# A decoder layer with 32 routed experts: the second block of a large expert set one unit behind the first, and the tokens of the next expert turned in two places

## The chip, the cores and the metric

The kernel runs on one core of a Trainium2 chip. The metric is the device time of one execution in microseconds (us); the change is made to a kernel of 1811.78 us (median of three runs).

## What is computed

One layer over 512 tokens of 1024 features: a mixer (gated DeltaNet and differential attention), a top-4-of-32 mixture of experts, and a gated embedding, each followed by a layer norm. Only the mixture is touched. Each expert that a token chose is a clamped SwiGLU:

```python
hgu = xb @ w_gu[e] + b_gu[e]                     # 1024 -> 2048
gate = jnp.minimum(hgu[:, :D_FF], 7.0)
up = jnp.clip(hgu[:, D_FF:], -7.0, 7.0)
act = (up + 1.0) * gate * jax.nn.sigmoid(1.702 * gate)
return act @ w_down[e] + b_down[e]               # 1024 -> 1024
```

The result is scaled by the token's gate and added to the token's row. How many tokens an expert has depends on the data.

## The kernel before, in words

**Units.** The weights of an expert are twelve units of 1 MB: 0 to 7 of `w_gu` (two row halves for each of four column blocks), 8 to 11 of `w_down`. Twelve raw buffers `mr` form a ring that SP fills (`mload`, L838); a buffer is loaded again when its unit has been split. ACT rounds a unit to its high part (`hi_of`, L1204, tile `mh`), DVE takes the rest (`lo_of`, L1209, tile `ml`); four pairs of such tiles form a second ring. `ahead(u)` (L1211) issues `hi` of unit u+3 and `lo` of unit u+2. PE multiplies the token tile by both parts.

**Forms.** The count of an expert's tokens picks one of three bodies at run time: `few` (L1243, up to 64 tokens, 8 matmuls of 512 columns per unit), `many` (L1279, up to 128, 12 matmuls), `over` (L1306, up to 256: 12 matmuls for the first block of 128 tokens and 12 for the second). Each body is a generator in five pieces (q = 0 to 4), so that common code can stand between them; the pieces hold the units 0 to 9, and `last_units` (L1359), common to the forms, holds units 10 and 11. The main loop is at L1627 to 1644.

**Tokens.** In piece q = 0 of expert e the common code scatters the rows of expert e-1 (`add_y`, L1229, two indirect DMAs of `yt` into `acc`, issued by POOL), makes the table of the token numbers of expert e+1 (`find`, L1215), gathers its rows into `xg` (indirect DMA of POOL, L1131) and makes the one-hots of expert e+2 on POOL (`one_hot`, L1108, eight instructions). In `last_units`, between units 10 and 11, `load_x` (L1220) turns `xg` on PE (two halves of four transposes, L1138, into the banks PT) and splits each half into a high part (ACT, L1143) and a low part (DVE, L1144), into the tiles `xa`. There are three `xa` tiles for four uses; `turned(e, i)` picks them in turn, i = 0 and 1 the tokens, i = 2 and 3 the activations.

**`few`.** Its two token tiles are first rearranged by POOL (two casts, L1248, which unit 0 and unit 1 wait for, and a clearing, L1249). At j = 5 and 9 the activation is formed on DVE (L1161, L1162) in `sT`, a part of the tile `ovg`, and split by ACT (L1263) and DVE (L1264); unit 10 uses what j = 9 made. Between the two, `ahead` is issued.

**`over`.** The body starts with the gather of the second block's rows into `ovg`. The second block runs two units behind the first (k = j - 2), with its own banks OV. Its tokens are turned behind the first block's unit 2 (`more_x`, L1167), its activations behind units 8 and 10 (into PT). `hi` and `lo` of unit j+2 are issued behind the matmuls of iteration j. At the end ACT empties OV into `ovg` (`more_y`, L1191) and POOL scatters it.

**Queues.** The kernel is scheduled by hand: the order of the code is the order in each engine's queue, and an engine that waits holds all that is behind it. POOL's queue per expert before: casts and clearing (in `few`), two scatters (the second waits until the first has landed), the gather of `xg`, the one-hots.

Of the kernel before, what the change touches and what calls it, by code (L numbers as in the profile page):

```python
# [15 lines left out]
AF = mybir.ActivationFunctionType  # L16
# [8 lines left out]
NE = 32  # L25
# [11 lines left out]
def build(ctx, tc, x, p, positions, w_in, conv_w, a_log, dt_bias, gdn_norm_w,  # L37
# [1111 lines left out]
    def split_T(src, dst, scale=None, ps=None):  # L1149

        turn4(src, ps)
        parts(ps, dst, scale)

    C7 = 11.914 / (1.0 + math.exp(-11.914))
    SW = 1.702
# [4 lines left out]
    def act_of(s, ps, a):  # L1160
        V.tensor_scalar(ps, ps, -6.0, 8.0, op0=OP.max, op1=OP.min)  # L1161
        V.scalar_tensor_tensor(a, s, C7, ps, op0=OP.min, op1=OP.mult)  # L1162
# [48 lines left out]
    def ahead(u):  # L1211
        hi_of(u + 3)
        lo_of(u + 2)
# [3 lines left out]
        table(e, oh, PT[1], idx, (0, 5) if e else (0, 2))  # L1217
        gather_rows(idx[0][:, 0:1], xg)

    def load_x(e):  # L1220
        for h in range(2):
            split_T(xg[:, h * 512:(h + 1) * 512], turned(e, h), ps=PT[h])

    def evac_y(e):
        if e >= 0:
# [17 lines left out]
    def few(e):  # L1243

        u0 = 12 * e
        x, aT = [turned(e, 0), turned(e, 1)], [turned(e, 2), turned(e, 3)]
        for t in x:
            G.tensor_copy(t[:, 0, :, 64:128], t[:, 1, :, 0:64])  # L1248
        G.tensor_scalar(aT[1][:, 1], aT[1][:, 0], 0.0, None, op0=OP.mult)  # L1249
        for j in range(10):  # L1250
            m, i = divmod(j, 2)
            prev = (m - 1) // 2
            if j and i == 0:
                A.activation(sb[(m - 1) % 2], PG[(m - 1) % 2], AF.Copy)
            ps = PT[(m - 1) % 2][:, 0:256].rearrange("p (a b) -> p a b", a=4)
            if j in (3, 7):
                silu(ps, sT)
            if j in (5, 9):
                act_of(sT, ps, sT)
            ahead(u0 + j)  # L1260
            if j in (5, 9):
                a = aT[prev]
                A.activation(a[:, 0, :, 0:64], sT, AF.Copy, scale=1.0 / SW)  # L1263
                V.scalar_tensor_tensor(a[:, 0, :, 64:128], sT, 1.0 / SW, a[:, 0, :, 0:64], op0=OP.mult, op1=OP.subtract)  # L1264
            hl = pairs[(u0 + j) % PAIRS]
            if j < 8:
                acc_, lhs, b = PG[m % 2], x[i], (lhs_bias(e, m // 2, 64), bias[:, m % 2, :])
            else:
                acc_, lhs, b = PY[i], aT[0], (lhs_bias(e, i, 64), dbias)
            mm_unit2(acc_, lhs, hl, j >= 8 or i == 0)  # L1270
            if j >= 8 or i == 0:
                T.matmul(acc_[0:64], *b, start=False, stop=False, skip_group_check=True)
            if j in (2, 4, 6, 8):
                for d in range(4):
                    T.matmul(ps[:, d], sb[(m - 1) % 2][:, d * 128:(d + 1) * 128], fold, start=True, stop=True)  # L1275
            if i:
                yield
# [27 lines left out]

    def over(e):  # L1306

        u0 = 12 * e
        x, aT = [turned(e, 0), turned(e, 1)], [turned(e, 2), turned(e, 3)]
        idx = tabs[e % 3]  # L1310
        pair = lambda j: pairs[(u0 + j) % PAIRS]
        gather_rows(idx[0][:, 1:2], ovg)
        for j in range(14):
            m, i = divmod(j, 2)
            prev = (m - 1) // 2
            k = j - 2
            if j == 0:
                ahead(u0)
            if j == 1:
                lo_of(u0 + 3)  # L1320
            if j in (2, 6):
                silu(PG[0], sb[prev])
            if j in (4, 8):
                act_of(sb[prev], PG[1], sb[prev])
            if j in (5, 9):
                parts(PT[prev], aT[prev], 1.0 / SW)
            if j in (4, 6, 8, 10):
                more_act((j - 4) // 2)
            if j == 9:
                parts(PT[0], x[1], 1.0 / SW)  # L1330
            if j == 11:
                parts(PT[1], ovT[0], 1.0 / SW)
            if j < 8:
                if i == 0:
                    mm_bias(PG[m % 2], e, m % 2, m // 2)
                mm_unit(PG[m % 2], x[i], pair(j), False, i == 1)
            elif j < 10:
                T.matmul(PY[i], lhs_bias(e, i), dbias, start=True, stop=False, skip_group_check=True)
                mm_unit(PY[i], aT[0], pair(j), False, False, skip_group_check=True)
            if j in (4, 8):  # L1340
                turn4(sb[prev], PT[prev])
            if j == 8:
                turn4(yt[:, 0:512], PT[0])
            if j == 2:
                more_x()
            if k >= 0:
                more_mm(e, k, ovT[i] if k < 8 else x[1] if k < 10 else ovT[0], pair(k))
            if j == 10:
                turn4(yt[:, 512:1024], PT[1])
            if 2 <= j < 11:  # L1350
                hi_of(u0 + j + 2)
            if 2 <= j < 10:
                lo_of(u0 + j + 2)
            if j >= 12:
                more_y(i, idx)
            if j in (1, 3, 5, 7, 13):
                yield

    def last_units(e):  # L1359
        u0, a = 12 * e, turned(e, 3)  # L1360
        for i in range(2):
            ahead(u0 + 10 + i)
            mload(u0 + 12 + i + RAWS)
            mm_unit(PY[i], a, pairs[(u0 + 10 + i) % PAIRS], False, True, skip_group_check=True)
            if i == 0 and e + 1 < NE:
                load_x(e + 1)

    def count(e, engines=ENG):
        return nc.values_load(cnt[0:1, e:e + 1], engines=engines)
# [239 lines left out]
        "d3 h3 q3 v3 W3 x3 y3 "  # L1609
    ).split()  # L1610

    one_hot(0, V)
    find(0)
    gate_parts()
    G.memset(ovg, 0.0)
    hi_of(0)
    hi_of(1)
    for i in range(2):
        lo_of(i)
        mload(i + RAWS)  # L1620
    hi_of(2)
    load_x(0)
    table(0, oh, PT[1], tabs[0], (2, 5))
    one_hot(1)
    words = [nc.values_load(forms[0:1, i:i + 1], engines=ENG, min_val=0, max_val=4 ** 11 - 1) for i in range(3)]

    for e in range(NE):  # L1627
        form = (words[e // 11] >> (2 * (e % 11))) & 3
        bodies = few(e), many(e), over(e)
        evac_y(e - 1)  # L1630
        for q in range(5):
            with tc.If(form == 2) as rest:
                next(bodies[0])
            with rest.Else():
                with tc.If(form == 1) as rest:
                    next(bodies[1])
                with rest.Else():
                    next(bodies[2])
            for i in range(2):
                mload(12 * e + 2 * q + 2 + i + RAWS)  # L1640
            if q == 0:
                add_y(e - 1)
                next_tables(e)
        last_units(e)
    tail()

# [21 lines left out]
```

## Time and profile before

| | us |
|---|---|
| median of three runs (1808.31 to 1812.39) | 1811.78 |
| the profiled execution | 1810.29 |
| its span | 1807.7 |
| one-hots on POOL, 248 instructions | 387.4 |
| `lo` on DVE, 389 instructions | 889.0 |
| `hi` on ACT, 389 instructions | 739.1 |

PE was busy 90% of the span, DVE 75%, ACT 60%, POOL 45%. The routed experts run from about 412 us to 1712 us of the span; 19 of them are `few`, 10 `many` and 3 `over`, as the counts of the groups' instructions show. Shares of the whole span hide that the forms differ, so the reading goes by stretches of single experts, and in them by the order of each queue: in a row of the trace, the bracket at its end gives the idle time of that engine just before the instruction and what ended it. Matmuls overlap in the pipeline, so a group of twelve is read from the start of the first to the start of what follows.

### The profile page before, as it was taken

To read this page: it belongs to the slowest core of one execution; us is meant where nothing else is said; L and a number is where in the kernel's file an instruction comes from. 1 tells how busy PE (TensorE), PEld (TensorE's weight loads), DVE (VectorE), ACT (ScalarE), POOL (GpSimd) and SP (SyncE) were. 2 spreads that over 40 slices of the span, in tenths; PEclk is the share of its full clock that TensorE was granted. 3 is DMA by queue.
4 is the path that set the end of the run, shared out by engine and by line. 5 is a ranking of instruction groups with operands and counts; after the bars stand their busy time and mean duration, and the time that the engine had idled before them with its cause. 6 is when DMAs were issued, how large, how long until landed. Compare 5 with 4: busy or idle time off the path is not lost.

```text
span 1807.7 us, 26591 instructions
## 1 busy us (share of the span) xinstructions
PE 1632.9 (90%) x8408; PEld 1331.4 (74%) x8408; DVE 1361.5 (75%) x1671; ACT 1084.3 (60%) x1152; POOL 814.6 (45%) x490
## 2 busy tenths in 40 slices
PE   8999889958989989989999899998999999899966
PEld 6889866846767768777887677777777777777755
DVE  6656686756449888997886477999899897468867
ACT  4463354336348767886775366878787685367722
POOL 0031210135225776686566056658767576024304
PEclk9999997968999989999999999999999999999988
DMA  7212401567549999999999389999999999479621
GB/s 240 58 44 64 111 13 30 211 234 268 182 134 362 378 360 355 367 382 358 356 351 335 118 270 366 359 355 379 379 378 377 368 362 372 147 233 368 209 72 47
DMA packets 255778, 467.94 MB, mean 259 GB/s; under 512 B 27820, under 2 KB 47198, under 8 KB 255476
## 3 DMA queue, kind: packets, MB, share of 16 engines
q1 hardware_dynamic: 237844, 437.37, 67.6%
q0 software_dynamic: 15328, 21.13, 4.8%
q10 hardware_dynamic: 2304, 5.51, 0.9%
q8 instruction: 178, 2.92, 0.7%
q14 instruction: 124, 1.02, 0.2%
HBM read 456.61 MB, written 41.81 MB: 276 GB/s over the span
## 4 chain that ended last, share of the span: by engine, by line
PE 36%; DVE 13%; issue 11%; DMA 8%; ACT 6%; POOL 1%; DVEq 0%; ACTq 0%; SPq 0%; POOLq 0%
PE pg L1068 14%; PE py L1068 10%; DVE ml L1209 9%; PE ov L1068 6%; ACT mh L1204 4%; DMA mr<-in_w_gu_dram 4%; DMA acc<-yt,idx 3%; PE pt L1138 2%; DMA mr<-in_w_down_dram 1%; PE pt L1275 1%; PE pg L1075 1%; PE pg L1079 1%; ACT yt L1227 1%; DVE pt L1161 1%; PE py L1075 1%
## 5 line engine op out<-in xcount | busy, mean ns | idle before, releaser
L1209 DVE TENSOR_TENSOR ml<-mr,mh 128x2048 fp32r<-128x2048 f32 x389 | 889.0, 2324 | 140.0 <-ACT mh L1204 96.7
L1204 ACT ACTIVATE mh<-mr 128x2048 fp32r<-128x2048 f32 x389 | 739.1, 1917 | 165.3 <-issue 61.3
L1108 POOL TENSOR_SCALAR oh<-slots,rkm 128x64 bf16<-128x64 bf16 x248 | 387.4, 1579 | 5.6 <-PE pt L1116 4.3
L1127 POOL DMA_INDIRECT acc<-yt,idx x64 | 161.1, 2518 | 325.8 <-DMA acc<-yt,idx 196.3
L1068 PE MATMUL py<-mh,xa 128*128 128x512 f32 x736 | 252.2, 426 | 60.6 <-DVE xa L1264 26.6
L1068 PE MATMUL pg<-mh,xa 128*128 128x512 f32 x864 | 268.2, 392 | 0.0
L1075 PE MATMUL pg<-mh,xa 128*128 128x512 f32 x608 | 247.9, 408 | 9.3 <-POOL xa L1248 8.8
L1075 PE MATMUL pg<-ml,xa 128*128 128x512 f32 x608 | 241.6, 397 | 0.0
L1068 PEld LDWEIGHTS py<-mh,xa 128*128 128x128 f32 x736 | 145.3, 205 | 104.1 <-ACT mh L1204 46.3
L1068 PEld LDWEIGHTS pg<-mh,xa 128*128 128x128 f32 x864 | 161.7, 188 | 33.4
L1068 PE MATMUL pg<-ml,xa 128*128 128x512 f32 x432 | 168.8, 391 | 0.0
L1068 PE MATMUL py<-ml,xa 128*128 128x512 f32 x368 | 154.1, 419 | 0.0
L1075 PEld LDWEIGHTS pg<-mh,xa 128*128 128x128 f32 x608 | 115.5, 190 | 36.7 <-POOL xa L1248 8.9
L1075 PEld LDWEIGHTS pg<-ml,xa 128*128 128x128 f32 x608 | 115.4, 190 | 26.1 <-DVE ovg L1162 3.4
L1143 ACT ACTIVATE xa<-pt 128x512 fp32r<-128x512 f32 x68 | 37.3, 596 | 148.1 <-PE pt L1138 133.3
L1144 DVE TENSOR_TENSOR xa<-pt,xa 128x512 fp32r<-128x512 f32 x68 | 44.0, 687 | 103.0 <-ACT xa L1143 102.9
L1068 PEld LDWEIGHTS pg<-ml,xa 128*128 128x128 f32 x432 | 81.1, 188 | 17.3
L1127 POOL DMA_INDIRECT acc<-ovg,idx x3 | 10.6, 3543 | 177.1 <-ACT ovg L1191 177.1
L1068 PEld LDWEIGHTS py<-ml,xa 128*128 128x128 f32 x368 | 75.0, 204 | 17.4
L1068 PE MATMUL ov<-mh,ovT 128*128 128x512 f32 x256 | 84.1, 412 | 0.0
L1248 POOL CAST xa<-xa 128x256 fp32r<-128x256 f32 x38 | 49.3, 1298 | 55.8 <-DVE xa L1144 55.8
L1249 POOL TENSOR_SCALAR xa<-xa 128x512 fp32r<-128x512 f32 x19 | 65.1, 3424 | 0.0
(452 smaller groups left out, 2801.0 us busy)
## 6 DMA issues: line engine op xcount, KB each, us to landing
mr<-in_w_gu_dram SPq DMA_DIRECT2D x256, 1024.0 KB, 10.3
mr<-in_w_down_dram SPq DMA_DIRECT2D x125, 1024.0 KB, 11.5
raw<-in_w_in_dram SPq DMA_DIRECT2D x14, 1024.0 KB, 5.4
raw<-in_w_out_dram SPq DMA_DIRECT2D x4, 1024.0 KB, 7.4
mr<-in_ple_gate_w_dram SPq DMA_DIRECT2D x4, 1024.0 KB, 9.4
mr<-in_w_down_dram ACTq DMA_DIRECT2D x3, 1024.0 KB, 7.5
xs<-in_x_dram SPq DMA_DIRECT2D x4, 512.0 KB, 4.6
xr<-in_x_dram SPq DMA_DIRECT2D x4, 512.0 KB, 5.5
```

Of the source, the lines that this page charges most:

```text
L1068: T.matmul(ps, lhs[:, a, k, :], w[:, k, :], start=first and k == 0 and a == 0 and w is hi, stop=last and k == 3 and w is lo, **kw)
L1075: T.matmul(ps, lhs[:, 0, k, :], w[:, k, :], start=first and k == 0 and w is hl[0], stop=not first and k == 3 and w is hl[1], skip_group_ch ...
L1079: T.matmul(ps, lhs_bias(e, par), bias[:, t, :], start=start, stop=False)
L1108: eng.tensor_scalar(oh[:, t, c], slots[:, c], r[:, t, e:e + 1], None, op0=OP.is_equal)
L1127: G.indirect_dma_start(out=acc, out_offset=bass.IndirectOffsetOnAxis(ap=at, axis=0), in_=src, in_offset=None, bounds_check=S - 1, oob_is_e ...
L1138: T.transpose(ps[:, d], src[:, d * 128:(d + 1) * 128], ident)
L1143: A.activation(dst[:, 0], ps, AF.Copy)
L1144: V.tensor_sub(dst[:, 1], ps, dst[:, 0])
L1204: A.activation(pairs[uid % PAIRS][0], raw[uid % RAWS], AF.Copy)
L1209: V.tensor_tensor(lo, raw[uid % RAWS], hi, op=OP.subtract)
L1248: G.tensor_copy(t[:, 0, :, 64:128], t[:, 1, :, 0:64])
L1249: G.tensor_scalar(aT[1][:, 1], aT[1][:, 0], 0.0, None, op0=OP.mult)
```

## The change

- `load_x` is gone. `x_turn` and `x_part` take its halves apart: the first half of the next tokens is turned and split behind piece q = 3 (unit 7), the second is turned at the head of `last_units`; ACT's part of it follows the first `ahead` there, DVE's the second.
- In `few`, ACT's and DVE's split of the activations stand ahead of `ahead`.
- In `over`, the second block runs one unit behind (k = j - 1); its tokens are turned behind the first block's unit 0; its activations go through the banks PG; the last four units of the second block stand at the end of j = 9, ahead of `last_units`. `hi` and `lo` of unit j+2 stand ahead of the matmuls of iteration j.
- The gather of `ovg` leaves `over` and stands in common code, at the end of `last_units` for every expert but the last, and once before the loop.
- Before the loop, the clearing of `ovg` and `gate_parts` stand first, the table's second part comes ahead of the turning of the tokens, and the one-hots of expert 1 are made by DVE.

```diff
-    def load_x(e):
-        for h in range(2):
-            split_T(xg[:, h * 512:(h + 1) * 512], turned(e, h), ps=PT[h])
+    def x_turn(e, h):
+        if e < NE:
+            turn4(xg[:, h * 512:(h + 1) * 512], PT[h])
+    def x_part(e, h, k):
+        if e < NE:
+            ps, d = PT[h].rearrange("p (a b) -> p a b", a=4), turned(e, h)
+            if k == 0:
+                A.activation(d[:, 0], ps, AF.Copy)
+            else:
+                V.tensor_sub(d[:, 1], ps, d[:, 0])
...
             if j in (5, 9):
+                a = aT[prev]
                 act_of(sT, ps, sT)
-            ahead(u0 + j)
-            if j in (5, 9):
-                a = aT[prev]
                 A.activation(a[:, 0, :, 0:64], sT, AF.Copy, scale=1.0 / SW)
                 V.scalar_tensor_tensor(a[:, 0, :, 64:128], sT, 1.0 / SW, a[:, 0, :, 0:64], op0=OP.mult, op1=OP.subtract)
+            ahead(u0 + j)
...
-        gather_rows(idx[0][:, 1:2], ovg)
-        for j in range(14):
+        beyond = lambda k: more_mm(e, k, ovT[k % 2 if k < 8 else k // 2 - 4], pair(k))
+        for j in range(10):
...
+            if j == 0:
+                hi_of(u0 + 3)
+            elif j > 1:
+                hi_of(u0 + j + 2)
+            lo_of(u0 + j + 2)
...
-            if j == 2:
+            if j == 7:
+                turn4(yt[:, 0:512], PG[0])
+            if j == 0:
                 more_x()
...
+            else:
+                beyond(j - 1)
+            if j == 9:
+                turn4(yt[:, 512:1024], PG[1])
+                parts(PG[1], ovT[1], 1.0 / SW)
+                hi_of(u0 + 12)
+                for k in (9, 10, 11):
+                    beyond(k)
+                    if k > 9:
+                        more_y(k - 10, idx)
...
     def last_units(e):
         u0, a = 12 * e, turned(e, 3)
         for i in range(2):
+            if i == 0:
+                x_turn(e + 1, 1)
             ahead(u0 + 10 + i)
+            x_part(e + 1, 1, i)
             mload(u0 + 12 + i + RAWS)
             mm_unit(PY[i], a, pairs[(u0 + 10 + i) % PAIRS], False, True, skip_group_check=True)
-            if i == 0 and e + 1 < NE:
-                load_x(e + 1)
+        if e + 1 < NE:
+            gather_rows(tabs[(e + 1) % 3][0][:, 1:2], ovg)
...
+    G.memset(ovg, 0.0)
+    gate_parts()
     one_hot(0, V)
     find(0)
-    gate_parts()
-    G.memset(ovg, 0.0)
+    gather_rows(tabs[0][0][:, 1:2], ovg)
...
-    load_x(0)
-    table(0, oh, PT[1], tabs[0], (2, 5))
-    one_hot(1)
+    table(0, oh, PT[0], tabs[0], (2, 5))
+    one_hot(1, V)
+    for h in range(2):
+        x_turn(0, h)
+        for k in range(2):
+            x_part(0, h, k)
...
+            if q == 3:
+                x_turn(e + 1, 0)
+                for i in range(2):
+                    x_part(e + 1, 0, i)
```

POOL's queue from the end of one expert to the start of the next, before (the scatter of `ovg` is in the branch of `over`, the casts in that of `few`):

```order
L1127 DMA acc<-ovg,idx_3892 512x1024
L1635 UNCONDITIONAL_BRANCH
L1632 REGISTER_ALU x2
L1632 COMPARE_AND_BRANCH
L1248 COPY xa_3881<-xa_3881 128x4x64
L1248 COPY xa_3882<-xa_3882 128x4x64
L1249 TENSOR_SCALAR xa_3881<-xa_3881 128x512
```

And with the change:

```order
L1127 DMA acc<-ovg,idx_3890 512x1024
L1650 UNCONDITIONAL_BRANCH
L1131 DMA ovg<-h1d,idx_3891 128x1024
L1647 REGISTER_ALU x2
L1647 COMPARE_AND_BRANCH
L1258 COPY xa_3882<-xa_3882 128x4x64
L1258 COPY xa_3883<-xa_3883 128x4x64
L1259 TENSOR_SCALAR xa_3882<-xa_3882 128x512
```

The gather of `ovg` now stands outside the branches, between the last thing POOL does for one expert and the casts of the next.

PE's queue in `over` where the second block's tokens are turned, before (`pg_3872` is the bank of the first block's units 2 and 3, `xa_3881` its first token tile):

```order
L1068 MATMUL pg_3872<-mh,xa_3881 128x512 x2
L1068 MATMUL pg_3872<-ml,xa_3881 128x512
L1138 MATMUL ov_3877<-ident,ovg 128x128 x4
L1138 MATMUL ov_3878<-ident,ovg 128x128 x4
L1079 MATMUL ov_3877<-bias,selb 128x512
L1068 MATMUL ov_3877<-mh,ovT_3887 128x512 x2
L1068 MATMUL ov_3877<-ml,ovT_3887 128x512
```

And with the change (`pg_3871` is the bank of units 0 and 1):

```order
L1068 MATMUL pg_3871<-mh,xa_3881 128x512 x2
L1068 MATMUL pg_3871<-ml,xa_3881 128x512
L1138 MATMUL ov_3877<-ident,ovg 128x128 x4
L1138 MATMUL ov_3878<-ident,ovg 128x128 x4
L1068 MATMUL pg_3871<-mh,xa_3882 128x512 x2
L1068 MATMUL pg_3871<-ml,xa_3882 128x512
```

The transposes moved from behind unit 2 to behind unit 0, and a unit of the first block now stands between them and the first unit of the second block.

DVE's queue in `few` at j = 9, before:

```order
L1209 TENSOR_TENSOR ml<-mr,mh 128x2048
L1161 TENSOR_SCALAR pt_3876<-pt_3876 128x256
L1162 SCALAR_TENSOR_TENSOR ovg<-ovg,pt_3876 128x256
L1209 TENSOR_TENSOR ml<-mr,mh 128x2048
L1264 SCALAR_TENSOR_TENSOR xa_3882<-ovg,xa_3882 128x4x64
```

And with the change (the first row is the low part of the next tokens' first half):

```order
L1232 TENSOR_TENSOR xa_3883<-pt_3875,xa_3883 128x512
L1647 REGISTER_ALU x2
L1647 COMPARE_AND_BRANCH
L1209 TENSOR_TENSOR ml<-mr,mh 128x2048
L1161 TENSOR_SCALAR pt_3876<-pt_3876 128x256
L1162 SCALAR_TENSOR_TENSOR ovg<-ovg,pt_3876 128x256
L1272 SCALAR_TENSOR_TENSOR xa_3882<-ovg,xa_3882 128x4x64
L1209 TENSOR_TENSOR ml<-mr,mh 128x2048
```

The split of the activations (L1264, now L1272) changed places with a `lo`, and a part of the next tokens stands ahead of the piece.

## Rows read from the trace of the kernel before

**Rows 1.** Busy time by stretch: stretch, its us, then each engine's, clock, DMA share, GB/s.
```profile
412.25:537.23 124.98, 113.12 (x498) 90.49 (x499) 63.62 (x56) 57.30 (x51) 38.31 (x26) 0.92 0.57 194
537.23:680.99 143.76, 131.98 (x634) 104.92 (x633) 125.12 (x101) 110.33 (x97) 98.15 (x55) 0.93 1.02 361
718.33:824.03 105.70, 96.88 (x476) 76.86 (x475) 93.91 (x76) 82.83 (x74) 75.06 (x41) 0.95 1.03 370
...
861.35:898.71 37.36, 36.58 (x176) 29.84 (x175) 32.64 (x26) 26.99 (x22) 23.27 (x11) 1.00 1.02 357
936.08:1056.77 120.69, 109.06 (x500) 87.91 (x499) 69.21 (x59) 58.98 (x54) 41.54 (x28) 0.96 0.66 228
970.92:1056.77 85.85, 76.69 (x342) 62.20 (x341) 38.12 (x34) 31.45 (x30) 17.10 (x14) 0.96 0.52 175
1056.77:1166.64 109.87, 101.38 (x492) 81.53 (x491) 94.97 (x76) 82.16 (x69) 72.19 (x38) 0.95 1.01 354
1203.92:1374.16 170.24, 157.09 (x792) 125.28 (x791) 155.59 (x126) 137.92 (x122) 125.30 (x69) 0.98 1.04 373
1448.87:1603.37 154.50, 139.86 (x658) 112.21 (x657) 100.47 (x84) 86.62 (x77) 65.61 (x40) 0.97 0.77 270
```
**Rows 2.** Timeline of POOL in expert 8, a `few`: start, us, engine, line, what.
```profile
751.87 0.40 POOL L1248 CAST xa<-xa 128x256 fp32r<-128x256 f32 x1 [1.56 <-DVE xa L1144]
752.47 2.30 POOL L1248 CAST xa<-xa 128x256 fp32r<-128x256 f32 x1 [0.20 <-DVE xa L1144]
...
773.24 11.91 POOL L1108 TENSOR_SCALAR oh<-slots,rkm 128x64 bf16<-128x64 bf16 x8
785.12 0.40 POOL L1248 CAST xa<-xa 128x256 fp32r<-128x256 f32 x1
```
**Rows 3.** The line of the gathers: ns min/median/max of issue, first and last start.
```profile
L1131 POOL DMA_INDIRECT xg<-h1d,idx x32: 1046/1736/3154, 392.4 to 1658.1; - x32
L1131 POOL DMA_INDIRECT ovg<-h1d,idx x3: 1086/1096/2292, 442.8 to 1515.8; - x3
```
**Rows 4.** The tile `ovg`, its six transfers (three gathers, three scatters).
```profile
DMA to landing us min/median/max: 7.5/9.3/10.2
```
**Rows 5.** Timelines of PE and DVE about unit 10 of experts 8 and 9.
```profile
780.13 0.70 PE L1068 MATMUL py<-mh,xa 128*128 128x512 f32 x2 [2.27 <-DVE xa L1264]
...
815.19 1.19 PE L1068 MATMUL py<-mh,xa 128*128 128x512 f32 x2 [3.67 <-issue]
...
813.61 0.41 DVE L1264 SCALAR_TENSOR_TENSOR xa<-ovg,xa 128x256 fp32r<-128x256 f32 x1
```
**Rows 6.** The chain of work, units 10 and 11 of expert 9: start, us, what.
```profile
815.19 5.46 PE py L1068 x12
...
821.60 2.74 PE py L1068 x12
```
**Rows 7.** Timeline of PE in expert 14, an `over`: first and last of three such waits.
```profile
996.20 0.66 PE L1138 MATMUL pt<-ident,s 128*128 128x128 f32 x4 [2.47 <-DVE s L1162]
...
1038.93 0.96 PE L1138 MATMUL pt<-ident,yt 128*128 128x128 f32 x4 [2.47 <-DVE yt L1162]
```
**Rows 8.** Timeline of PE at unit 11 of expert 6, a `many`.
```profile
712.05 0.70 PE L1068 MATMUL py<-mh,xa 128*128 128x512 f32 x2 [0.77 <-DVE ml L1209]
```
**Rows 9.** Timeline of POOL at the end of expert 28, an `over`.
```profile
1597.23 3.55 POOL L1127 DMA_INDIRECT acc<-ovg,idx  x1 [58.80 <-ACT ovg L1191]
1607.90 2.64 POOL L1127 DMA_INDIRECT acc<-yt,idx  x1 [7.12 <-DMA acc<-ovg,idx]
```
**Rows 10.** Timelines of POOL, PE and DVE before the first expert.
```profile
392.37 2.48 POOL L1131 DMA_INDIRECT xg<-h1d,idx  x1 [3.20 <-DVE idx L1122]
...
398.14 0.99 POOL L1615 MEMSET ovg<- 128x1024 f32 x1
...
412.25 0.80 PE L1075 MATMUL pg<-mh,xa 128*128 128x512 f32 x1 [8.78 <-POOL xa L1248]
...
389.33 1.38 DVE L1108 TENSOR_SCALAR oh<-slots,rkm 128x64 bf16<-128x64 bf16 x8
```

More of the change, by code (lines that the diff above doesn't have):

```diff
@@ L1311, in over @@
         pair = lambda j: pairs[(u0 + j) % PAIRS]
-        gather_rows(idx[0][:, 1:2], ovg)
-        for j in range(14):
+        beyond = lambda k: more_mm(e, k, ovT[k % 2 if k < 8 else k // 2 - 4], pair(k))
+        for j in range(10):
             m, i = divmod(j, 2)
             prev = (m - 1) // 2
[L1316 to L1320, printed above, removed]
             if j in (2, 6):
@@ L1324, in over @@
                 act_of(sb[prev], PG[1], sb[prev])
+            if j in (3, 5, 7, 9):
+                more_act((j - 3) // 2)
+            if j == 8:
+                parts(PG[0], ovT[0], 1.0 / SW)
             if j in (5, 9):
                 parts(PT[prev], aT[prev], 1.0 / SW)
[L1327 to L1332, printed above, removed]
+            if j == 0:
[3 more added lines that the diff above has]
+            lo_of(u0 + j + 2)
             if j < 8:
@@ L1336, in over @@
                 mm_unit(PG[m % 2], x[i], pair(j), False, i == 1)
-            elif j < 10:
+            else:
                 T.matmul(PY[i], lhs_bias(e, i), dbias, start=True, stop=False, skip_group_check=True)
@@ L1341, in over @@
                 turn4(sb[prev], PT[prev])
-            if j == 8:
-                turn4(yt[:, 0:512], PT[0])
-            if j == 2:
+            if j == 7:
+                turn4(yt[:, 0:512], PG[0])
+            if j == 0:
                 more_x()
[L1346 to L1356, printed above, removed]
+            else:
+                beyond(j - 1)
[7 more added lines that the diff above has]
+                        more_y(k - 10, idx)
+            if i:
                 yield
```

## Prediction

> **What bounds the kernel now.** The times below are set against the profiled execution: 1810.29 us, of which 1807.7 us are the span; the median of the three runs shown is 1811.78 us. I read the windows by group of experts first, then the engine queues inside one expert of each form. Call the forms F (`few`, 19 experts), M (`many`, 10) and O (`over`, 3: experts 1, 14 and 28). By expert number the order is F O FFFF M FFF MMM F O F M F M FFFFF MM FF O MM F.
>
> No engine is the bound throughout. An M takes 37.36 us, in which PE is busy for 36.58 us at the full clock: PE sets it [rows 1]. An O takes 85.85 us with PE idle for 9.2 us and a mean granted clock of 0.96 [rows 1]. At 0.96, about 0.08 of the stretch ran at 1.2 GHz instead of 2.4 GHz, which cost half of 6.9 us; so PE alone would need 85.85 - 9.2 - 3.4 = 73.3 us. In a row of F the reader is to look at POOL: from its first cast at 751.87 to the same cast of the next expert at 785.12 are 33.25 us, and the second one begins with no idle time ahead of it [rows 2]. POOL's queue is full there, and its period is the F's best time. Slower F (143.76 us for four, 35.9 each) run with a clock of 0.93 [rows 1]. What lowers it is seen at unit 10: PE waited 3.67 us [rows 5], and the twelve matmuls behind the wait took 5.46 us where the next twelve took 2.74 [rows 6]. A wait of 2.27 us at the same place was not followed by this [rows 5]. The weights come at 361 to 373 GB/s in the groups of F [rows 1], and none of PE's waits in the rows is released by them.
>
> **The change part by part.**
>
> *Tokens turned early.* The eight transposes of the next tokens leave the gap between units 10 and 11; four stand behind unit 7, four ahead of unit 10. Their number, and that of the ACT and DVE parts, is unchanged: 0 us of work. What goes is head-of-line blocking: ACT and DVE stood before their halves until PE had done unit 10. One new lateness: DVE now does the second half's part behind `lo` of units 12 and 13, and POOL's second cast waits for it. An F that follows pays about 1 us at its unit 1, since a cast beside a running `lo` takes 2.30 us where the one without takes 0.40 [rows 2].
>
> *M.* PE's one wait, 0.77 us for `lo` of unit 11 [rows 8], is covered: four transposes and an earlier DVE queue lie ahead. Bounds 0 and 0.77; I take 0.77. Nine M outside the groups below: -6.9 us.
>
> *`ahead` behind the split in `few`.* The split that unit 10 waits for ran at 813.61, behind a `lo` of 2.3 us [rows 5]; it now stands ahead of that. DVE instead waits some 0.6 us for ACT's half, so I count a wait of 1 us at unit 10 in place of 2.27 to 3.67, and no fall of the clock there. PE's F is then 33.25 - 2.27 + 1 = 32 us, and 32.5 us with the late cast.
>
> *The second block's gather in common code.* It was issued three times; now it is issued 32 times, once before the loop and then behind unit 11 of each expert but the last, for F and M with no valid row. On POOL it stands between the one-hots and the next expert's casts. Of its three issues before, the two right behind one-hots took 1.09 and 1.10 us, the third 2.29; the tokens' gather takes 1.74 us in the median, 1.05 at least and 3.15 at most [rows 3]. I take 1.1 us, the nearest row, and 0.15 us ahead of it; so F to F costs POOL 33.25 + 1.25 = 34.5 us, with 34.4 and 36.5 as ends. (Where PE, having waited 2.5 us, runs a while at 1.2 GHz, its F is 32 + 2.7 = 34.7 us, so that this adds little to POOL's period; it counts for the last F of a row.) F cannot get to 32.5 us next to another F; only the last F of a row can. An M has no casts, so PE does not wait for POOL there.
>
> The Trainium skill (SBUF — State Buffer, "Who interferes with whom") says that a DVE instruction with two SBUF inputs blocks a GpSimd instruction that reads SBUF, and infers that descriptor generation is not blocked by it. The two casts agree (0.40 and 2.30); the gathers of 1.74 us in F do not, but the 1.1 us at this very place do. With 1.74 us the ten F-to-F steps would cost 6 us more in all.
>
> *O.* The old order puts `lo` behind the second block's unit, so the transposes of the activations wait three times 2.47 us (996.20, 1022.07, 1038.93) [rows 7]; now `hi` and `lo` of unit j+2 begin a whole double unit (5.5 us) ahead and the second block's transposes have a unit behind them. These waits and the loss of clock go: 73 us of PE work remain. But the tokens are wanted behind the *first* unit, 2.7 us into O, where they were wanted three units in. Landing takes 7.5 to 10.2 us from issue, median 9.3 [rows 4]. Behind an F, POOL comes to the gather only 33.5 us after that F's start. F of 32 us, issue at 33.5, landing at 42.8: PE stands from 34.7 to 42.8, and loses some 2.7 us of clock [rows 6]. F and O of experts 13 and 14: 42.8 + 73 = 116 us against 120.69 [rows 1], -4.7 us. Experts 26 to 28 (F, F, O): 0.4 + 34.5 + 33.3 + 9.3 + 73 = 150.5 against 154.50, -4 us.
>
> The Trainium skill (DMA: Bandwidth & Descriptors, "Anatomy of one DMA — SWDGE (gpsimd) path") fits 2.0 us plus bytes by 436 GB/s, which is an estimate of 3.2 us for 512 KB. The trace has 7.5 us at least [rows 4]; with 3.2 us the wait here would be 2 us, and the first rival below would come near.
>
> *Behind O.* The gather overwrites `ovg`, so it waits until the scatter of O's second block has landed. That scatter took 3.55 us, and the next on it began only 7.12 us later, 10.7 us after its start [rows 9]; O's last two units cover 5.5 us. So the casts come about 6.5 us after O's end. An F behind O pays this and 2.7 us of clock. Experts 2 to 5: 6.5 + 3 × 34.5 + 32.5 + 1.4 (half a clock loss, an even chance) = 143.9 against 143.76. Experts 15 to 17 (F M F): 6.9 + 32.5 + 2.7 + 36.6 + 32 = 110.7 against 109.87. An M behind O pays 0.5 us.
>
> *The other rows of F.* Experts 7 to 9: 0.4 + 2 × 34.5 + 33.9 = 103.3 against 105.70. Experts 19 to 23: 0.4 + 4 × 34.5 + 33.9 = 172.3 against 170.24. Together -0.3 us.
>
> *The start.* PE waits 8.78 us for the first cast, since POOL makes the one-hots of expert 1 first [rows 10]. On DVE such a set takes 1.38 us, while DVE would wait for the gather. Against it, the gate parts and the clearing of `ovg`, 4.3 us from 394.85 to 399.13, now stand ahead of POOL's first gather, where POOL was idle for 3.20 us [rows 10]: 1 us later. So -7.8 us; bounds -4.5 and -8.8. Then expert 0: 31 us, 2.7 us of slow clock at its beginning and 1 us of waiting, and expert 1: 73 us, 3.2 us until its tokens land (the gather waits for DVE's last `lo` of the body, 3.4 us before O) and 1.4 us of clock. 34.7 + 77.6 = 112.3 against 124.98 from the first matmul on [rows 1], -12.7 us.
>
> **Sum:** M -6.4, into O -8.7, behind O +0.9, F rows -0.3, start -7.8, experts 0 and 1 -12.7: -35 us. 1810.3 - 35 = **1775 us**.
>
> **The rivals.**
>
> *POOL is no obstacle*: the gather without a row costs nothing, and the tokens land in time. Speaks for it: nothing is moved for 29 of the 32. Against: 1.09 us is time of issue, not of transfer, and 7.5 us is the shortest landing [rows 3, 4]. F to F 33 us (10 × 1.5 = 15), both late O without the wait and its clock (2 × 10), the two F behind an O half as late (8): 1775 - 43 = 1732 us.
>
> *The O keeps its waits in another form.* The gather lands at 10.2 us or later, PE stays at 1.2 GHz for longer than the 5.46 us seen, and some of the waits of 2.47 us come back at other double units. Of -21 us for O (experts 1, 14, 28) some -5 remain: 1791 us, up to 1800.
>
> *Slower: POOL's queue becomes the bound of every F.* Place: the gather ahead of the casts. If it holds POOL as long as a scatter does (3.55 us [rows 9]) and not 1.1, the ten F-to-F steps, the two into a late O and the two from an O to an F each cost 2.4 us more, and all four rows' last F and both late O start at 1.2 GHz for certain (6 × 1.4 more): 1775 + 14 × 2.4 + 8 = 1817 us. It decides from 3.1 us per gather on: 14 × 2.0 + 8 is the whole gain. Against: no gather of `ovg` behind one-hots took more than 1.10 us.
>
> *The change does less than it says*: M keeps its wait (7 us) and the start gains 4.5 us and not 7.8: 1785 us, inside the range.
>
> **How the numbers follow.** The forecast, 1758 to 1790 with the bounds of the gather (1.05 to 1.74 us), of the landing (7.5 to 10.2 us) and of the start: 0.6, with the case of less effect in it. POOL no obstacle: 0.15. O's waits kept: 0.12, of it 0.06 within 0.2% of the time before, if some waits that I have not seen come on top. Slower: 0.10, and 0.03 for waits that I have not seen, on that side. The range, 1742 to 1803, takes in the second of these whole and the nearer part of the first; what is left out is the far part of the first and the slower case. A change of 0.2% (3.6 us) is about what a measurement can tell from none: faster 0.82, same 0.06, slower 0.12.
>
> **What would show it.** Right: M at 36.6 us with no wait at unit 11; F next to F at 34.5 us with POOL never idle from cast to cast; PE's wait in O at the transposes of `ovg`, released by their gather, for experts 14 and 28 (about 8 us) and hardly for expert 1; a wait of 6 to 7 us at the first unit behind O, released by POOL; the first matmul of expert 0 near 404.5 us. Wrong: F to F at 33 us, or PE's waits of 2.47 us still in O, or a gather of 3 us.

## The result and the profile after

The changed kernel takes **1876.85 us** (median of 4 runs, 1869.73 to 1884.18) against 1811.55 us before: a ratio of 1.0364, 95% interval 1.0319 to 1.041. It is 65 us slower; the forecast was 1775 us. The profiled execution ran 1873.57 us with a span of 1871.8 us, 64.1 us more than the span before.

First the busy time by stretch, the same groups of experts as in [rows 1], cut where ACT begins to empty the last unit's banks into `yt`; the row for 429.81 is expert 1 alone.

```profile
core 0: us, PE busy (x) PEld busy (x) DVE busy (x) ACT busy (x) POOL busy (x), PEclk, DMA share, GB/s
397.20:502.20 105.00, 104.03 (x495) 84.73 (x496) 68.40 (x58) 59.38 (x51) 35.83 (x24) 0.98 0.67 234
429.81:502.20 72.39, 72.39 (x341) 59.30 (x340) 39.15 (x34) 31.82 (x29) 16.14 (x12) 1.00 0.58 195
502.20:672.72 170.52, 130.76 (x635) 104.38 (x633) 124.31 (x101) 110.25 (x97) 90.99 (x61) 0.90 0.88 307
708.87:833.00 124.13, 97.38 (x477) 78.08 (x476) 93.84 (x76) 82.75 (x73) 61.93 (x44) 0.90 0.90 317
869.38:905.95 36.57, 36.57 (x176) 29.88 (x175) 32.50 (x26) 27.14 (x22) 19.85 (x12) 1.00 1.03 364
942.30:1059.92 117.62, 104.89 (x500) 85.06 (x499) 70.06 (x59) 59.48 (x53) 37.94 (x26) 0.96 0.67 234
1059.92:1180.67 120.75, 101.85 (x492) 82.21 (x491) 94.24 (x76) 82.38 (x70) 68.97 (x43) 0.92 0.95 329
1216.85:1430.36 213.51, 163.80 (x792) 130.59 (x791) 156.84 (x126) 138.07 (x121) 105.59 (x74) 0.90 0.87 308
1503.11:1661.72 158.61, 137.97 (x658) 111.20 (x657) 101.79 (x84) 87.09 (x77) 58.84 (x41) 0.96 0.74 258
```

The O is what it was meant to be: expert 1 takes 72.39 us with PE busy in all of it, at a clock of 1.00. An M takes 36.57 us, again with PE never idle. The rows of F are the loss: five F went from 170.24 to 213.51 us, the clock there from 0.98 to 0.90, the weights from 373 to 308 GB/s. Three groups of the page say where:

```profile
L1138 PE MATMUL pt<-ident,xg 128*128 128x128 f32 x256 | 47.7, 319 | 139.1 <-DMA xg<-h1d,idx 135.6
L1232 DVE TENSOR_TENSOR xa<-pt,xa 128x512 fp32r<-128x512 f32 x64 | 43.8, 685 | 162.1 <-ACT xa L1230 161.9
L1108 POOL TENSOR_SCALAR oh<-slots,rkm 128x64 bf16<-128x64 bf16 x240 | 237.1, 1004 | 1.3
```

PE stands 135.6 us ahead of the transposes of the next tokens, until the gather of `xg` has landed. ACT and DVE stand with it, since their parts of the tokens wait for PE. The view of the tile `xg` counts PE's waits and tells its landing:

```profile
  PE pt L1138: 135.6, 17
DMA to landing us min/median/max: 5.2/7.9/9.3
```

One of the 17 waits is the start's (8.2 us; it was 8.6 us before), one is in expert 29, an M behind an O (4.7 us); the other fifteen are in fifteen F, 8.2 us each. The timelines of POOL and PE in expert 4, one of these, show one of them:

```profile
595.80 5.34 POOL L1127 DMA_INDIRECT acc<-yt,idx  x1 [0.17 <-issue]
607.52 2.57 POOL L1127 DMA_INDIRECT acc<-yt,idx  x1 [6.38 <-DMA acc<-yt,idx]
610.40 1.39 POOL L1131 DMA_INDIRECT xg<-h1d,idx  x1 [0.30 <-issue]
611.82 4.66 POOL L1108 TENSOR_SCALAR oh<-slots,rkm 128x64 bf16<-128x64 bf16 x8
...
608.75 0.39 PE L1075 MATMUL pg<-ml,xa 128*128 128x512 f32 x1
618.02 1.08 PE L1138 MATMUL pt<-ident,xg 128*128 128x128 f32 x4 [8.89 <-DMA xg<-h1d,idx]
618.76 0.78 PE L1075 MATMUL py<-mh,xa 128*128 128x512 f32 x1
619.33 0.63 PE L1075 MATMUL py<-ml,xa 128*128 128x512 f32 x1
```

The expert began at 587.59. PE has done unit 7 at 609.1, 21.5 us later. POOL issues the gather only at 610.40, behind the casts, two scatters and the wait between them; it lands at 618.0. Behind the wait a matmul of 512 columns takes 0.63 us where it took 0.39. In the windows of this expert:

```profile
597.00:608.00 11.00, 11.00 (x59) 9.05 (x59) 9.94 (x8) 9.11 (x9) 4.62 (x2) 1.00 1.02 359
618.00:625.50 7.50, 7.47 (x29) 6.17 (x30) 3.96 (x5) 3.56 (x5) 0.00 (x0) 0.68 0.05 19
```

A clock of 0.68 over 7.5 us is 4.8 us at the lower of the two levels, 1.2 GHz: 2.4 us lost. Read in the same way, the fifteen F lost 1.5 to 2.7 us behind the wait, 2.0 us in the mean. They take 42.5 us each; less 8.2 and 2.0 us they would take 32.3 us, an estimate. The one-hots fell from 387.4 us (248 instructions) to 237.1 us (240): in these F they lie beside a DVE that stands during the wait.

That the tokens would come late could be read from the kernel before. Its timelines of POOL and PE in expert 8, which began when [rows 2] begins, have these rows:

```profile
771.46 1.73 POOL L1131 DMA_INDIRECT xg<-h1d,idx  x1 [0.30 <-issue]
...
772.44 0.39 PE L1075 MATMUL pg<-ml,xa 128*128 128x512 f32 x1
772.67 0.40 PE L1075 MATMUL py<-mh,xa 128*128 128x512 f32 x1
...
782.96 1.03 PE L1138 MATMUL pt<-ident,xg 128*128 128x128 f32 x8
```

The gather went out at 771.46, one microsecond before PE was through unit 7, and PE asked for its tokens 11.5 us after the issue. Moved to behind unit 7, it asks 1.2 us after it.

### The profile page after: what moved, and what is told of

Read it like the earlier page. It is cut to its first block, busy times and chain, and to the rows that moved or that the text cites. A ratio compares the mean times of both kernels' runs of the same rounds, so it can differ in the third digit from the quotient of the medians.

```text
span 1871.8 us, 26590 instructions
## 1 busy us (share of the span) xinstructions
PE 1617.3 (86%) x8408; PEld 1325.0 (71%) x8408; DVE 1364.6 (73%) x1679; ACT 1088.3 (58%) x1152; POOL 734.1 (39%) x511
## 5 line engine op out<-in xcount | busy, mean ns | idle before, releaser
L1075 PE MATMUL pg<-mh,xa 128*128 128x512 f32 x608 | 250.9, 413 | 43.8 <-POOL xa L1258 24.8
L1127 POOL DMA_INDIRECT acc<-yt,idx x64 | 174.7, 2730 | 283.6 <-DMA acc<-yt,idx 181.9
L1108 POOL TENSOR_SCALAR oh<-slots,rkm 128x64 bf16<-128x64 bf16 x240 | 237.1, 1004 | 1.3
L1068 PE MATMUL py<-mh,xa 128*128 128x512 f32 x736 | 232.2, 397 | 0.8 <-DVE xa L1272 0.8
L1068 PEld LDWEIGHTS pg<-mh,xa 128*128 128x128 f32 x864 | 161.2, 188 | 33.9 <-POOLq L1647 0.7
L1138 PE MATMUL pt<-ident,xg 128*128 128x128 f32 x256 | 47.7, 319 | 139.1 <-DMA xg<-h1d,idx 135.6
L1068 PEld LDWEIGHTS py<-mh,xa 128*128 128x128 f32 x736 | 137.3, 190 | 28.6 <-ACT xa L1271 1.3
L1131 POOL DMA_INDIRECT ovg<-h1d,idx x32 | 55.7, 1742 | 239.8 <-ACT mh L1204 164.7
L1068 PE MATMUL py<-ml,xa 128*128 128x512 f32 x368 | 144.8, 393 | 0.0
L1138 PEld LDWEIGHTS pt<-ident,xg 128*128 128x128 f32 x256 | 34.5, 162 | 155.4 <-issue 142.1
L1068 PE MATMUL ov<-mh,ovT 128*128 128x512 f32 x304 | 94.5, 392 | 0.0
L1258 POOL CAST xa<-xa 128x256 fp32r<-128x256 f32 x38 | 62.8, 1656 | 52.4 <-DVE xa L1232 29.5
```

The source lines that it names most:

```text
L1068: T.matmul(ps, lhs[:, a, k, :], w[:, k, :], start=first and k == 0 and a == 0 and w is hi, stop=last and k == 3 and w is lo, **kw)
L1075: T.matmul(ps, lhs[:, 0, k, :], w[:, k, :], start=first and k == 0 and w is hl[0], stop=not first and k == 3 and w is hl[1], skip_group_ch ...
L1108: eng.tensor_scalar(oh[:, t, c], slots[:, c], r[:, t, e:e + 1], None, op0=OP.is_equal)
L1127: G.indirect_dma_start(out=acc, out_offset=bass.IndirectOffsetOnAxis(ap=at, axis=0), in_=src, in_offset=None, bounds_check=S - 1, oob_is_e ...
L1131: G.indirect_dma_start(out=dst, out_offset=None, in_=h1d, in_offset=bass.IndirectOffsetOnAxis(ap=at, axis=0), bounds_check=S - 1, oob_is_e ...
L1138: T.transpose(ps[:, d], src[:, d * 128:(d + 1) * 128], ident)
```

## The experiments

Theory 1: the early turn puts PE's queue ahead of the landing of `xg`, and that is the whole loss. Theory 2: the gathers of `ovg`, 32 in place of 3, hold POOL and so the F. Theory 3: the second half of the tokens, split late, holds the F. Theory 4, formed on the way: without the wait, POOL's queue bounds the F.

All results in one table. The three columns of forms are means over the experts of each form in the profiled execution, from one first emptying into `yt` to the next (expert 0 from its first matmul). The ratio is that to the kernel before on the same chip.

| | median us | ratio, 95% interval | F | M | O |
|---|---|---|---|---|---|
| before | 1811.55 | | 35.1 | 37.3 | 86.3 |
| after | 1876.85 | 1.0364 [1.0319, 1.041] | 41.4 | 37.0 | 73.1 |
| e1 turn late | 1779.11 | 0.9806 [0.9757, 0.9855] | 35.7 | 36.3 | 77.2 |
| e2 gather first | 1870.05 | 1.0348 [1.0285, 1.0411] | 38.4 | 36.6 | 89.1 |
| e3 before, early turn | 1908.45 | 1.0532 [1.0483, 1.0581] | 39.4 | 38.5 | 86.6 |
| e4 `ovg` in `over` | 1889.68 | 1.0438 [1.0392, 1.0485] | 41.7 | 37.2 | 73.0 |
| e5 before, new `over` | 1770.03 | 0.9775 [0.9753, 0.9796] | 34.7 | 37.4 | 74.2 |
| e6 = e1 and e4 | 1755.96 | 0.9697 [0.9678, 0.9717] | 34.9 | 36.3 | 77.0 |
| e7 = e6, one-hots on DVE | 1730.35 | 0.9551 [0.9535, 0.9567] | 33.8 | 36.3 | 72.7 |
| e8 = e2 and e4, one-hots on DVE | 1765.90 | 0.9754 [0.9719, 0.9788] | 33.9 | 36.4 | 84.9 |
| e9 gather between the scatters | 1795.32 | 0.9915 [0.9888, 0.9941] | 36.3 | 36.4 | 79.2 |
| e10 = e9 and e4, one-hots on DVE | 1747.97 | 0.9658 [0.9629, 0.9687] | 34.1 | 36.4 | 77.7 |
| e11 after, one-hots on DVE | 1861.91 | 1.029 [1.0252, 1.0327] | 40.1 | 37.9 | 73.3 |

**e1: the changed kernel with the tokens turned in the old place.**

```diff
-            if i == 0:
-                x_turn(e + 1, 1)
             ahead(u0 + 10 + i)
-            x_part(e + 1, 1, i)
             mload(u0 + 12 + i + RAWS)
             mm_unit(PY[i], a, pairs[(u0 + 10 + i) % PAIRS], False, True, skip_group_check=True)
+            if i == 0:
+                for h in range(2):
+                    x_turn(e + 1, h)
+                    for k in range(2):
+                        x_part(e + 1, h, k)
...
-            if q == 3:
-                x_turn(e + 1, 0)
-                for i in range(2):
-                    x_part(e + 1, 0, i)
```

> The changed kernel, with the next tokens turned where they were turned before (both halves between units 10 and 11). Theory 1: what the change lost is PE standing behind unit 7 of 17 F until the gather of xg has landed (135.6 us in the trace of the changed kernel, and the fall of the clock behind it). Then the 17 F go from 42.5 us each to 33.5 to 34.5 us, no matmul L1138 on xg waits for the gather, and the time is 1873.6 - 17 x 8.5 = 1729 us, plus up to 25 us if the tokens of the second block now come late behind the shorter F of experts 13 and 27: 1725 to 1755 us. Theory 2: the gather of ovg, now issued 32 times on POOL, is what holds F; then this edit gives back little: 1840 us or more. Theory 3: the late second half (DVE's part of it behind lo, POOL's second cast waits for it) is what holds F: this edit cannot tell it from theory 1, the next one can.

1779.11 us, 98 us less than the changed kernel: the loss of 65 us is gone and 33 us more, and theory 2 falls. But the time is 24 us above the upper end of what theory 1 gave. The view of PE's waits shows what is late next:

```profile
PE pg L1075 <- POOL xa L1258: 45.2, 11, 7.1
PE pt L1138 <- DMA xg<-h1d,idx: 11.9, 2, 11.1
PE ov L1138 <- DMA ovg<-h1d,idx: 11.2, 2, 8.6
```

Of the wait for `xg`, 11.9 us are left, 11.1 of them at the start. In its place PE waits eleven times for POOL's casts at the first units of an F; POOL's timeline in experts 3 and 4 has the reason, and PE's the wait:

```profile
574.30 16.19 POOL L1108 TENSOR_SCALAR oh<-slots,rkm 128x64 bf16<-128x64 bf16 x8
590.65 2.61 POOL L1131 DMA_INDIRECT ovg<-h1d,idx  x1 [0.16 <-issue]
593.27 0.75 POOL L1258 CAST xa<-xa 128x256 fp32r<-128x256 f32 x2
...
593.82 0.77 PE L1075 MATMUL pg<-mh,xa 128*128 128x512 f32 x1 [7.05 <-POOL xa L1258]
```

With PE and DVE running on, the one-hots of this expert take 16.19 us (11.91 in [rows 2]), and POOL goes from them to the gather and the casts without a stop. That is theory 4. The ten F that follow an F take 36.7 us in the mean.

**e2: the gather of `xg` ahead of the scatters, the early turn kept.** `add_y(e - 1)` moves from ahead of `next_tables(e)` into it:

```diff
-    def next_tables(e):
+    def next_tables(e, done):
         if e + 1 < NE:
             find(e + 1)
+        add_y(done)
```

> The changed kernel with one swap on POOL: the table and the gather of xg stand ahead of the two scatters of expert e-1, not behind them. The tokens are still turned behind unit 7 and ahead of unit 10. Theory 1: the gather then goes out some 10 us into an F instead of 20 to 23 us, lands before unit 7 is done (20.6 us), and PE's 17 waits (135.6 us) go: F at 34 to 35.5 us (the late second cast still costs 1.7 us at unit 0), time 1745 to 1775 us. Theory 2 (the gathers of ovg) and theory 3 (the late second half): nothing of either is touched, so F stays above 40 us and the time above 1850 us.

1870.05 us, hardly better: an expectation missed, and by the time alone the run would speak for theories 2 and 3. PE's waits say that the mechanism did what theory 1 says, and that another wait took its place:

```profile
PE pg L1075 <- issue: 93.4, 12, 8.3
PE pt L1138 <- DVE s L1162: 23.6, 3, 8.1
PE ov L1138 <- DMA ovg<-h1d,idx: 16.1, 2, 8.6
PE pt L1138 <- DMA xg<-h1d,idx: 8.2, 1, 8.2
```

Only the start's wait for `xg` is left (8.2 us). But PE now stands twelve times at the first unit of an F. POOL's and PE's timelines show one of these:

```profile
588.76 16.37 POOL L1108 TENSOR_SCALAR oh<-slots,rkm 128x64 bf16<-128x64 bf16 x8
605.29 1.10 POOL L1131 DMA_INDIRECT ovg<-h1d,idx  x1 [0.16 <-issue]
606.40 0.75 POOL L1259 CAST xa<-xa 128x256 fp32r<-128x256 f32 x2
...
606.91 0.77 PE L1075 MATMUL pg<-mh,xa 128*128 128x512 f32 x1 [8.30 <-issue]
```

The releaser reads "issue", but PE goes on half a microsecond after POOL's casts begin, and these stand behind late scatters and one-hots of 16.37 us. The three O take 89.1 us. In two of them PE waits 16.1 us in all for the gather of `ovg`, which stands behind late one-hots too; the eighth run shows what the 23.6 us are.

**e3: the kernel before with the early turn alone.** `x_turn` and `x_part` as in the change, `load_x` gone; `over`, `few`, the start and the gathers as before. (In the old `over` the tile that takes the next tokens' first half also holds the second block's activations, so that the values of the O and of the expert behind each differ.)

> The kernel before with the early turn alone (first half behind unit 7, second ahead of unit 10); over, few, the start and the gather of ovg as they were. Theory 1: this part alone makes the loss and more: F at 43 to 44 us where they took 33 to 36, nine M gain 0.8 us each; 1920 to 1955 us. Theory 2: no gather of ovg is added, so 1800 to 1820 us.

1908.45 us, 96 us more than the kernel before on the same chip: this part by itself makes the loss, and no gather of `ovg` was added. The expected 110 to 145 us were too much: F take 39.4 us and not 43 to 44, and the waits for `xg` come to 121.3 us in 19 places, the start's among them. The nine M other than expert 29 lost 0.7 us each and did not gain 0.8; PE waits there ahead of the second half for DVE, which I have not traced further.

**e4: the changed kernel with the gather of `ovg` at the head of `over`**, issued three times. The edit is the removal of the two calls of `gather_rows(..., ovg)` from common code and one line at the head of `over`.

> The changed kernel with the gather of ovg back at the head of over, issued three times and not 32. Theory 1: F keeps its 42 us; each O waits some 7 to 9 us behind its first unit for the tokens of its second block; 1873.6 + 3 x 8 = 1890 to 1905 us, less up to 10 us where F or M behind an O no longer wait for that gather. Theory 2: the 17 F lose at least 5 us each, so 1800 us or less in spite of the O.

1889.68 us: theory 2 falls again, F stay at 41.7 us. The O hardly waited for their tokens (73.0 us; PE stood 1.0 us in expert 28): with such slow F ahead, POOL reaches the head of `over` in experts 14 and 28 early and stands there for 11.4 and 10.5 us. So the time lies at the end of theory 1's range without the three waits that it was added up from: in this profile the first matmul comes 8.2 us later than in the changed kernel, F take 0.3 and M 0.2 us more.

**e5: the kernel before with the new `over` alone.**

> The kernel before with the new body of over alone (second block one unit behind, its activations through the banks PG, weights' parts ahead of the matmuls); the gather of ovg stays at its head, everything else is as before. Theory 1 (the new order is worth what the changed kernel's O show, 72.4 to 74.0 us against 85.8 to 87.4): expert 1 at 72 to 74 us; experts 14 and 28 come behind an F of 34 us, so that their tokens land late, as the prediction said, and take 80 to 83 us. 1811 - 13 - 2 x 5 = 1780 to 1792 us. Rival (the gain in O needed the slow F ahead of it or another part of the change): O stay above 83 us, 1800 us or more.

1770.03 us, less than the expected 1780 to 1792: O went from 86.3 to 74.2 us, and this part alone is worth 42 us. Expert 14 waited for its tokens only this long in PE's timeline, not some 8 us:

```profile
953.76 1.09 PE L1138 MATMUL ov<-ident,ovg 128*128 128x128 f32 x8 [1.35 <-DMA ovg<-h1d,idx]
```

The F ahead of it took 34.8 us. Where that F took 32.5 and 32.2 us (e1 and e6), PE waited 8.6 and 8.3 us and expert 14 took 82.5 and 82.7 us: 115 us for experts 13 and 14, where the prediction had 116.

**e6, e7: the late turn, the gather of `ovg` in `over`, then also the one-hots on DVE.** The edit of e7 against e6 is one word:

```diff
-            one_hot(e + 2)
+            one_hot(e + 2, V)
```

> The first experiment's kernel (tokens turned late) with the gather of ovg back at the head of over. Theory 4: with PE's wait for xg gone, F is bound by POOL's queue (casts, clearing, two scatters with a landing between them, gather, one-hots of 11.9 to 16.2 us, gather of ovg of 1.1 to 2.6 us); each F that follows an F then gains 1.2 to 2.6 us: 1779 - 11 x 2 = 1750 to 1768 us. Rival: POOL is not the bound, the gather without rows lies in idle time: 1775 to 1785 us.

> The kernel of the sixth run with the one-hots of expert e+2 on DVE (1.4 us for eight there, 11.9 to 16.2 us on POOL). Theory 4 (POOL's queue bounds F): PE stops waiting for POOL's casts and F falls from 35.7 us to what the weights' transfers allow, 33.2 us, the shortest F of the kernel before: 17 x 2.5 = 42 us less than the first experiment, 1725 to 1745 us. Rival (DVE, with 12 lo of 2.3 us and the one-hots, becomes the bound, or transfers do): F stays at 35 us or more, 1765 us or more.

1755.96 and **1730.35 us**, both inside the ranges of theory 4, but only e7 for the reason given. In e6 the ten F that follow an F should have gained 1.2 to 2.6 us each; they take 36.8 us in the mean, 36.7 us in e1. What e6 gained lies elsewhere: experts 2 and 15, the F behind an O, take 32.9 and 32.5 us in place of 40.4 each, since their casts no longer stand behind a gather that waits for the scatter of `ovg`, and the first matmul comes 8.9 us earlier in this profile. In five of the ten F next to an F, POOL now stands ahead of the casts for about as long as the gather took, until DVE has split the tokens; in expert 4:

```profile
578.73 0.40 POOL L1258 CAST xa<-xa 128x256 fp32r<-128x256 f32 x1 [2.66 <-DVE xa L1232]
```

So e6 does not show that the gather of `ovg` holds F next to F. e7 shows that the one-hots do. PE's wait for POOL's casts, 45.2 us in e1, is in e6 and in e7:

```profile
PE pg L1075 <- POOL xa L1258: 32.1, 6, 6.2
PE pg L1075 <- POOL xa L1258: 1.2, 1, 1.2
```

The ten F next to an F take 33.9 us in e7. It is the fastest of all kernels here, 4.5% below the kernel before. Its first two experts, and then four F, in the windows:

```profile
404.75:510.85 106.10, 104.65 (x497) 85.26 (x498) 70.65 (x75) 59.09 (x51) 16.68 (x10) 0.98 0.68 235
510.85:648.00 137.15, 125.12 (x634) 98.23 (x633) 130.18 (x133) 109.33 (x98) 51.40 (x23) 1.00 1.04 371
```

POOL is busy for 51 of 137 us, where it was 98 of 144 us in the same four F before [rows 1], the clock is 1.00, and the weights come at 371 GB/s, about the rate of the best F before [rows 1]. What bounds F now I have not tried; the weights' rate and DVE, busy for 130 of the 137 us, are both near.

**e8: as e7, but with the early turn and the gather ahead of the scatters.**

> The second experiment's kernel (early turn kept, gather of xg ahead of the scatters) with the gather of ovg at the head of over and the one-hots on DVE, so that POOL's queue is short. Theory 1 with theory 4: the early turn costs nothing by itself once xg has landed before unit 7 is done and POOL is not full; F at 33 to 34.5 us, no wait for xg, and the time within 15 us of the seventh run: 1725 to 1755 us. Rival (turning early is bad in itself, through the late second half and the casts behind it): 17 x 2 us and more over the seventh run, or F at 38 us and more: above 1765 us.

1765.90 us, above the expected 1725 to 1755 and, by the time alone, just in the rival's range. But F are at 33.9 us with the early turn, as with the late one (33.8 us): theory 3 falls as the cause of the loss, and where its tokens have landed and POOL has time the turn costs F next to nothing. (PE still waits for the late casts, 20.6 us in 18 places.) The missing 35 us are the three O (84.9 against 72.7 us). PE's waits and ACT's timeline in expert 1 show why:

```profile
PE pt L1138 <- DVE s L1162: 29.8, 3, 11.6
...
464.09 0.60 ACT L1158 ACTIVATE yt<-ov 128x512 f32<-128x512 f32 x1 [14.14 <-DMA acc<-yt,idx]
```

`over` keeps the second block's activations in `yt`, and the scatters that still read `yt` now stand behind the gather. In e7 the same wait of ACT is 4.30 us, and PE does not stand behind it.

**e9, e10: the gather between the two scatters; e11: the changed kernel with the one-hots on DVE.** In e9 the first scatter stands ahead of `find(e + 1)`, the second behind it; e10 adds e7's two edits. e11 has e7's one word against the changed kernel.

> The changed kernel with one move on POOL: the gather of xg stands between the two scatters of expert e-1 (where POOL otherwise waits for the landing of the first), one-hots on POOL and the gather of ovg in common code as in the changed kernel. Theory 1: the gather goes out some 12 us into an F, lands before unit 7, and PE's 135.6 us of waits for xg go; the scatters are not later than they were, so O stays at 72 to 74 us (in the second and eighth experiments it took 82 to 94 us). Theory 4: F is then bound by POOL's full queue, as in the first experiment, at 35 to 37 us: 1775 to 1800 us. Rival (the early turn costs by itself): F stays above 40 us, 1850 us or more.

> The ninth kernel with the one-hots on DVE and the gather of ovg at the head of over. Theory 1 with theory 4: the early turn kept, no wait for xg, POOL's queue short, O at 73 us: within 10 us of the seventh run's 1730 us, 1720 to 1740 us. Rival (the second half, turned late, costs F 1.5 us or more each): 1745 us or more.

> The changed kernel with the one-hots on DVE and nothing else. The one-hots stand behind the gather of xg in POOL's queue. Theory 1 (what counts is how far into an F the gather of xg is issued, behind casts and two scatters): the gather comes hardly sooner, PE still waits some 8 us in most F, F above 38 us: 1840 to 1875 us. Rival (POOL's queue is simply too long for an F): F falls to 34 us, 1750 us or less.

e9: 1795.32 us, 82 us less than the changed kernel by moving one DMA past another. F are 36.3 us, as theory 4 said, but O took 79.2 and not 72 to 74 us: the second scatter is still late, since the gather waits for its table (the same wait on `yt` is 8.95 us in expert 1), and PE waits 2.7 and 1.2 us for the gather of `ovg` in experts 14 and 28. e10: 1747.97 us, outside the expected 1720 to 1740 and in the rival's range, but not by the rival's cause: F take 34.1 us, 0.3 more than in e7, and O 77.7 us for the same wait on `yt` (8.7 to 9.9 us). e11: 1861.91 us, inside its range; with the one-hots gone from POOL's queue, PE still waits:

```profile
PE pt L1138 <- DMA xg<-h1d,idx: 106.8, 20, 8.7
```

The gather did come sooner than expected: the waits in the 17 F are 3.8 to 7.7 us, 5.3 us in the mean and not some 8. Still, most of the wait is left. So it is the gather's place in POOL's queue, behind the casts and two scatters, that makes most of the loss, and not the queue's length; the length decides what F cost once the gather is in time.

## Why the prediction was wrong

The forecast by its own groups, against the windows (negative is less time):

| part | forecast us | measured us |
|---|---|---|
| start, to the first matmul | -7.8 | -15.1 |
| experts 0 and 1 | -12.7 | -20.0 |
| 2 to 5 | +0.1 | +26.8 |
| 7 to 9 | -2.4 | +18.4 |
| 13 and 14 | -4.7 | -3.1 |
| 15 to 17 | +0.8 | +10.9 |
| 19 to 23 | +2.1 | +43.3 |
| 26 to 28 | -4.0 | +4.1 |
| nine M; expert 31; behind the loop | -6.4 | -1.9; -1.5; +2.1 |

- **The step that failed** is "Tokens turned early", costed at "0 us of work. What goes is head-of-line blocking". It looked at what stands behind the turn on ACT and DVE, and not at what the turn itself waits for. PE's transposes need the landing of `xg`; they were moved 10 us forward in an F and the gather was not. The cost is fifteen waits of 8.2 us, and 2.0 us of clock in the mean behind each: by estimate 153 us, of which the rest of the change gave back all but 65. e1 (undone: 98 us less), e3 (alone: 96 us more) and e9 (the gather moved instead: 82 us less) show it from three sides. The late cast, put at about 1 us for an F that follows, is a small part: PE waited 24.8 us for POOL's casts in 17 places, 1.5 us each.
- The same error ran through the rivals: the slower one was POOL's gather of `ovg` as the bound, and the waits "that I have not seen" had 0.03. e4 shows that the gather of `ovg` was not the loss.
- **F next to F, 34.5 us by POOL**: not to be seen in the changed kernel, where POOL waits. With the wait gone (e1), POOL does bound the F that follow an F, but at 36.7 us in the mean. The step built on one period, 33.25 us, among the shortest of the ten before (33.2 to 37.1 us, mean 34.8), and took the one-hots as 11.91 us, which took 16.19 us in the expert of e1 shown. e6 speaks against its price for the gather of `ovg`: without it these F are no shorter. PE's own F, forecast at 32 to 32.5 us, is 32.3 us by the estimate above and 32.2 us in the shortest F of e6 but the last expert.
- **O**: right in what it costs PE. 73 us of PE work were forecast, 72.4 to 74.0 us measured; the waits of 2.47 us [rows 7] are gone. The late tokens of experts 14 and 28 did not come in the changed kernel (PE stood 0.4 and 1.1 us there), since the slow F gave POOL the time; in e1 and e6 they came, in full in expert 14 and at 2.6 and 2.7 us in expert 28.
- **M**: right where nothing stands ahead: 36.1 to 36.6 us, 36.6 forecast. Expert 29, behind an O, took 43.4 us and not 37.1, since its gather of `xg` was late too.
- **Behind O**: the wait for POOL, forecast at 6.5 us, was 7.8 us in experts 2 and 15, the two F behind an O.
- **Start**: right in sign. The first matmul came 15 us earlier in this profile, 4.5 to 11.6 us earlier in the other kernels with this start and its gather (e1, e2, e9, e11), so that -7.8 lies among them.

## What to carry to other kernels

When a consumer is moved forward, read the issue and the landing of what it consumes in the same timeline, in every form of the body, before anything else: here two rows of the kernel before, 771.46 and 772.44, held the loss. A move that is free for one form (M, O) can cost another where the producer stands in a queue of its own. When such a wait goes, cost the next queue too: of the 147 us between the changed kernel and e7, 49 were still to be had behind e1. 26 of them came when the one-hots left POOL (e6 to e7). The other 23 came when the gather of `ovg` left common code (e1 to e6): 15 us in the two F behind an O, and 8.9 us at the start, which differs by as much between kernels that start alike.

## What was not expected of the hardware

The same eight one-hots took 1.38 to 1.79 us on DVE (e7, e8, e10, e11). On POOL they took from 4.65 us (after) to 17.98 us (e1). The windows of the set of 4.66 us shown above and of the set of 17.98 us:

```profile
611.82:616.48 4.66, 0.00 (x0) 0.00 (x0) 0.00 (x0) 0.00 (x0) 4.65 (x8) 0.59 1.04 374
790.90:808.90 18.00, 17.39 (x84) 13.86 (x83) 17.42 (x13) 15.65 (x15) 17.95 (x8) 1.00 1.05 381
```

The weights came at the same rate in both; DVE, ACT and PE stood in the first. What the length follows is DVE's `lo`: in the nine kernels with the one-hots on POOL, the 30 sets of the loop with no `lo` beside them took 4.65 to 5.15 us, the 60 sets with 12 us or more of `lo` beside them 14.75 to 17.98 us. No run changed `lo` alone. What a set costs on POOL can therefore not be taken over from one kernel to the next: 11.91 us [rows 2] became 16.19 us once DVE stood less. The issue of the gathers goes the same way: over all these runs, the 56 issues in the loop with no `lo` beside them held POOL for 1.00 to 1.13 us, the others for up to 7.62 us.

The median landing of `xg` was 7.9 us in the changed kernel and 7.8 us before, though five F drew 308 GB/s in the one and 373 GB/s in the other. These are medians over all gathers of a kernel, and no run changed the load alone, so whether a single landing follows the load is not shown.
